# Reordering the last matmuls of a 2D prefix-sum diagonal kernel, leaving out two small sums, and making its weights by integer shifts

## The chip, the cores and the metric

The kernel runs on one core of one Trainium2 chip. The metric is the device time of one execution in microseconds (us); a smaller one is better. Times are medians over several runs. A profile is taken of one execution of each kernel; in it a span is the time from the first to the last instruction, some 1.7 us less than the device time. Ratios are the mean time of one kernel's runs over the mean of the other's runs of the same rounds, so they are not quite the ratio of the medians quoted beside them.

## The reference

```python
B, H, W = 4, 4224, 4224
def reference(x):                         # x: float32 [B, H, W]
    ps = np.cumsum(np.cumsum(x, axis=1), axis=2)
    diag = np.diagonal(ps, axis1=1, axis2=2)
    return np.cumsum(diag, axis=1).astype(np.float32)
```

Each output is a weighted sum over the matrix, so every element has to be read once, and the work on each is small.

## The kernel before

It streams each matrix as strips of 768 rows through three buffers. The last 128 rows of the last matrix come last, as four blocks of 32 rows (`part_b`, blocks 0 to 3). TensorE gathers the contributions to the last 384 outputs in one row of PSUM, `fin`, by matmuls whose left side is a column of sums. `fin_e` holds block 3's share of the last 32 outputs.

```python
    w4_ps = psum_s.tile([P, P], FP32, name="fold")        # setup
    matmul(w4_ps, quarter, weights[:R, :P], start=True)
    weights4 = consts.tile([P, P], FP32, name="weights4")
    nc.vector.tensor_copy(out=weights4, in_=w4_ps)
    # ... (four matrices of strips) ...
        by = last.tile([P, P], FP32, name="by")           # block 0, by TensorE
        nc.scalar.copy(out=by, in_=by_ps)
        weigh(arows[:, 0:1], weights, 0, start=True)      # sums of 256 earlier rows
        weigh(arows[:, 1:2], weights, P)
        weigh(ones_col, by, M0)
        weigh(dtot, weights, M0)                          # diagonal block
        for k, ca in ((0, 512), (1, 448)):                # blocks 1 and 2
            act_sum(bsum[:, k, 0:1], part_b[:, k + 1, :ca])     # ScalarE
            pair_sum(bsum[:, k, 1:2], part_b[:, k + 1, ca:])    # VectorE
            if k == 1:
                finish(0, M0)          # add the first 256 results (VectorE reads fin)
            row_sums(btot[:, k : k + 1], bsum[:, k])            # combine the two sums
            weigh(btot[:, k : k + 1], weights4, M0 + (k + 1) * R)
        act_sum(esum[:, 0:1], part_b[:, 3, :320])         # block 3
        pair_sum(esum[:, 1:2], part_b[:, 3, 320:bcut])
        pair_sum(esum[:, 2:3], part_b[:, 3, bcut:])
        for k in (1, 0, 2):
            matmul(fin_e, esum[:, k : k + 1], weights4[:, :R], start=k == 1)
        finish(M0, GW)
        # ... output of yl ...
        nc.vector.tensor_add(out=ye, in0=fin_e, in1=yl[:, E0:])   # the last addition
        # ... output of ye ...
```

Of the kernel before, what the change touches and what calls it, by code (L numbers as in the profile page):

```python
# [8 lines left out]
FP32 = mybir.dt.float32  # L9
BF16 = mybir.dt.bfloat16  # L10
I32 = mybir.dt.int32
AX = mybir.AxisListType
ALU = mybir.AluOpType
# [4 lines left out]
def kernel(  # L18
# [14 lines left out]
    nc = tc.nc  # L33
# [3 lines left out]
    P = 128  # L37
# [11 lines left out]
    consts = ctx.enter_context(tc.tile_pool(name="consts", bufs=1))  # L49
# [4 lines left out]
    last = ctx.enter_context(tc.tile_pool(name="last", bufs=1))  # L54
# [3 lines left out]
    psum_s = ctx.enter_context(  # L58
        tc.tile_pool(name="psum_s", bufs=1, space=bass.MemoryType.PSUM)
    )  # L60
# [30 lines left out]
    def upper_mask(f):  # L91
# [19 lines left out]
        out=um1,  # L111
        in_=um1,
        compare_op=ALU.is_gt,
        fill=0.0,
        base=0,
        pattern=[[1, GW]],
        channel_multiplier=-1,
# [5 lines left out]
        out=ident,  # L123
        in_=ident,
        compare_op=ALU.is_equal,
        fill=0.0,
        base=0,
        pattern=[[-1, P]],
        channel_multiplier=1,
# [8 lines left out]
    def counted(name, rows, width, pieces):  # L138

        ti = consts.tile([P, GW], I32, name="counted")[:rows, :width]  # L140
        for c0, c1, base, step, cm in pieces:
            nc.gpsimd.iota(
                ti[:, c0:c1],
                pattern=[[step, c1 - c0]],
                base=base,
                channel_multiplier=cm,
            )
        tf = consts.tile([rows, width], FP32, name=name)
        nc.gpsimd.tensor_copy(out=tf, in_=ti)
        return tf  # L150
# [6 lines left out]
    def between_groups(name, turned):  # L157
# [25 lines left out]
    weights = counted("weights", P, GW, [(0, GW, 1, 1, -1)])  # L183
    nc.gpsimd.affine_select(
        out=weights,
        in_=weights,
        compare_op=ALU.is_ge,
        fill=0.0,
        base=0,
        pattern=[[1, GW]],  # L190
        channel_multiplier=-1,
# [1 line left out]


    R = P // 4
    quarter = consts.tile([R, P], FP32, name="quarter")
    nc.gpsimd.memset(quarter, 1.0)
    for base, step in ((0, 1), (3, -1)):
        nc.gpsimd.affine_select(  # L199
            out=quarter,  # L200
            in_=quarter,
            compare_op=ALU.is_ge,
            fill=0.0,
            base=base,
            pattern=[[step, P]],
            channel_multiplier=-4 * step,
        )

    ident_h = consts.tile([P, P], BF16, name="ident_h")
    nc.vector.tensor_copy(out=ident_h, in_=ident)  # L210
# [1 line left out]
    def matmul(o, lhsT, rhs, start=False):  # L212
        nc.tensor.matmul(  # L213
            o, lhsT=lhsT, rhs=rhs, start=start, stop=False, skip_group_check=True
        )

    w4_ps = psum_s.tile([P, P], FP32, name="fold")
    matmul(w4_ps, quarter, weights[:R, :P], start=True)
    weights4 = consts.tile([P, P], FP32, name="weights4")
    nc.vector.tensor_copy(out=weights4, in_=w4_ps)  # L220
    weights4_h = consts.tile([P, P], BF16, name="weights4_h")
    nc.vector.tensor_copy(out=weights4_h, in_=w4_ps)
    ones_col = consts.tile([P, 1], FP32, name="ones_col")
    nc.vector.memset(ones_col, 1.0)

# [5 lines left out]
    def act_sum(acc, src):  # L231
        w = src.shape[-1]
        dump = dumpool.tile([P, 2176], BF16, name="dump")
        nc.scalar.activation(  # L234
            out=dump[:, :w], in_=src, func=ACT.Copy, accum_out=acc
        )

    def row_sums(acc, src):
        nc.vector.reduce_sum(out=acc, in_=src, axis=AX.X)  # L239
# [3 lines left out]
    def pair_sum(acc, src):  # L243

        w = src.shape[-1] // 2
        pair = last.tile([P, 288], FP32, name=f"pair{len(pairs)}")
        pairs.append(pair)
        nc.vector.scalar_tensor_tensor(
            out=pair[:, :w],
            in0=src[:, :w],  # L250
            scalar=1.0,
            in1=src[:, w:],
            op0=ALU.mult,
            op1=ALU.add,
            accum_out=acc,
        )
# [27 lines left out]
    dtot = last.tile([P, 1], FP32, name="dtot")  # L284
# [9 lines left out]
    for b in range(B):  # L294
# [10 lines left out]
        def row_of(j):  # L305
            return (j + t0) % NG
# [59 lines left out]
        for h in range(2):  # L366
            ps = slice(h * HP, (h + 1) * HP)
            k = row_of(h)
            nc.vector.tensor_copy(  # L369
                out=r6[ps, k : k + 2 * ns : 2, :], in_=a6[ps, :, :, 1]  # L370
# [29 lines left out]
        if not whole:  # L400
# [9 lines left out]
            for sb, c0, c1 in (  # L410
# [8 lines left out]
                    out=part_b[:, sb, c0:c1],  # L419
                    in_=x[b, r0 : r0 + R, :TB].rearrange("r (k c) -> r k c", k=4)[  # L420
                        :, :, c0:c1
                    ],
# [21 lines left out]
        for i, src in enumerate((d, c12[:, 0, :])):  # L444
            nc.vector.tensor_tensor_scan(  # L445
                out=c12[:, i, :],
# [8 lines left out]
            out=out[b, : j1 * GW].rearrange("(g i) -> g i", i=GW),  # L455
            in_=c12[t0:NG, 1, :],
# [11 lines left out]
        arows = last.tile([P, 2], FP32, name="arows")  # L468
# [3 lines left out]
        M0 = 2 * P  # L472
# [5 lines left out]
        def weigh(rows, w, r0, start=False):  # L478

            matmul(fin[:, r0:], rows, w[:, : GW - r0], start=start)  # L480

        def finish(c0, c1):
            nc.vector.tensor_add(
                out=yl[:, c0:c1], in0=fin[:, c0:c1], in1=c12[0:1, 1, c0:c1]
            )
# [5 lines left out]
            matmul(by_ps, part_b[:, 0, c : c + P], weights4_h, start=c == 0)  # L491
        by = last.tile([P, P], FP32, name="by")
        nc.scalar.copy(out=by, in_=by_ps)
        weigh(arows[:, 0:1], weights, 0, start=True)
        weigh(arows[:, 1:2], weights, P)
        weigh(ones_col, by, M0)
        weigh(dtot, weights, M0)


        bsum = last.tile([P, 2, 2], FP32, name="bsum")  # L500
        btot = last.tile([P, 2], FP32, name="btot")
        for k, ca in ((0, 512), (1, 448)):
            act_sum(bsum[:, k, 0:1], part_b[:, k + 1, :ca])
            pair_sum(bsum[:, k, 1:2], part_b[:, k + 1, ca:])
            if k == 1:
                finish(0, M0)
            row_sums(btot[:, k : k + 1], bsum[:, k])
            weigh(btot[:, k : k + 1], weights4, M0 + (k + 1) * R)


        esum = last.tile([P, 3], FP32, name="esum")
# [3 lines left out]
        for k in (1, 0, 2):  # L515
# [3 lines left out]
            out=out[b, T0 : T0 + E0].unsqueeze(0), in_=yl[:, :E0]  # L519
# [34 lines left out]
```

## Time and profile before

| | before |
|---|---|
| device time, median of 3 runs | 668.09 us (667.10 to 669.24) |
| span in the profile (an execution of 667.37 us) | 665.7 us |
| busiest compute engine, VectorE | 334.6 us, 50% |
| VectorE's setup ends, first strip's work begins | 20.95 us, 34.84 us |
| ScalarE starts on block 3 | 662.46 us |
| the last addition starts | 663.50 us |

The page's first lines and the end of the timeline are shown in the prediction. (The GB/s row there stays near 219, half of the 429 GB/s that are read; this fits the strips being stored as bf16, half as wide as the float32 input.) What it tells in words of the setup is this part of the timeline (start, duration, engine, line, operation, and in brackets the idle time of that engine before it and what ended it):

```profile
16.53 0.64 POOL L199 TENSOR_SCALAR_AFFINE_SELECT quarter<-quarter 32x128 f32<-32x128 f32 x2
17.22 0.79 PE L213 MATMUL fold<-weights,quarter 32*128 32x128 f32 x2 [17.22 <-POOL quarter L199]
18.05 0.29 DVE L220 COPY weights<-fold 128x128 f32<-128x128 f32 x1 [5.45 <-PE fold L213]
34.84 2.56 DVE L329 TENSOR_TENSOR mu<-strip,um 128x4608 bf16<-128x4608 bf16 x1 [13.89 <-DMA strip<-in_x_dram]
```

The bracket of the last line is the point: VectorE has done its setup and stands idle for 13.89 us until the first strip lands.

In this document a "tail" is the time from ScalarE's start on block 3's first piece to the start of the last addition. That ScalarE instruction waits only for its data, so it marks when the transfer has delivered it; the tail is what computing adds after that. Before, it is 663.50 - 662.46 = 1.04 us.

### The profile page before, as it was taken

The numbers are of one execution on the slowest core, as the hardware profiler recorded it, in microseconds if no ns is written. First come the engines' busy times: TensorE is split into PE (matmuls) and PEld (weight loads), VectorE is DVE, ScalarE is ACT, GpSimd is POOL, SyncE is SP. The second block draws the span as 40 slices with busy tenths as digits, with TensorE's granted clock in tenths as the row PEclk, the third lists the DMA queues.
The fourth block names the chain that finished last, engine by engine and source line by source line (L and its number), as shares of the span: only waits on it lengthen the run. The fifth ranks groups of instructions, "written<-read, shape, count | busy, mean of one in ns | idle before, by whom it ended". The sixth has DMA issues, their size and how long they took to land.

```text
span 665.7 us, 2561 instructions
## 1 busy us (share of the span) xinstructions
PE 204.8 (31%) x979; PEld 98.2 (15%) x979; DVE 334.6 (50%) x166; ACT 140.3 (21%) x226; POOL 32.0 (5%) x61
## 2 busy tenths in 40 slices
PE   0081522403117143130221623404032264250427
PEld 0030211101003021110110311202011031120103
DVE  3161625456916153454782524436288333352867
ACT  0001121406300103040630020304063002030436
POOL 7000000000000000000000000000000000001000
PEclk9995857656558585675755957666565586766758
DMA  9999999999999999999999999999999999999998
GB/s 203 219 219 219 219 218 218 219 209 212 219 221 218 218 218 219 218 218 216 209 218 220 218 216 218 219 218 218 218 213 215 219 217 215 219 217 218 218 205 161
DMA packets 7670, 143.23 MB, mean 215 GB/s; under 512 B 702, under 2 KB 1002, under 8 KB 2154
## 3 DMA queue, kind: packets, MB, share of 16 engines
q0 software_dynamic: 7296, 142.47, 99.9%
q1 hardware_dynamic: 362, 0.61, 0.3%
q8 instruction: 7, 0.11, 0.1%
q14 instruction: 5, 0.04, 0.0%
HBM read 285.47 MB, written 0.07 MB: 429 GB/s over the span
## 4 chain that ended last, share of the span: by engine, by line
DVE 47%; another core or an unknown queue 44%; DMA 5%; PE 2%; issue 1%; DVEq 0%; POOLq 0%
DVE acc L239 29%; DVE mu L329 8%; DVE strip L330 8%; DMA strip<-in_x_dram 5%; PE d L213 1%; DVE c L445 1%; PE fold L213 1%; DVE pu L239 0%; PE fin L213 0%; DVE c L259 0%; DVE rows L369 0%; DVE acc L344 0%; PE carry_ps L213 0%; DVE carry L443 0%
## 5 line engine op out<-in xcount | busy, mean ns | idle before, releaser
L213 PE MATMUL d<-strip,sel 128*11 128x384 bf16 x603 | 138.6, 403 | 359.9 <-DMA strip<-in_x_dram 359.9
L234 ACT ACTIVATE dump<-strip 128x416 bf16<-128x416 bf16 (+8 forms) x112 | 128.4, 1146 | 521.9 <-DMA strip<-in_x_dram 519.2
L329 DVE TENSOR_TENSOR mu<-strip,um 128x4608 bf16<-128x4608 bf16 (+1 forms) x24 | 52.4, 2183 | 305.8 <-DMA strip<-in_x_dram 305.7
L239 DVE TENSOR_REDUCE acc<-strip 128x6 f32<-128x4608 bf16 (+6 forms) x23 | 196.0, 8523 | 0.8
L213 PEld LDWEIGHTS <-sel 128*11 128x11 bf16 x849 | 86.2, 102 | 504.7 <-issue 463.0
L213 PE MATMUL d<-mu,sel 128*11 128x384 bf16 x243 | 49.1, 355 | 45.8 <-DVE mu L329 45.8
L330 DVE TENSOR_TENSOR strip<-strip,mu 128x4608 bf16<-128x4608 bf16 (+1 forms) x24 | 52.4, 2183 | 1.0
L76 POOL DMA_DIRECT2D strip<-in_x_dram x24 | 16.5, 688 | 542.1 <-DVE acc L239 281.5
L234 ACT ACTIVATION_READ_ACCUMULATOR dump<-strip 128x1 f32 x112 | 20.9, 186 | 0.0
L213 PE MATMUL d<-ident,rows 128*11 128x128 f32 x24 | 5.2, 380 | 16.7 <-DVE rows L378 16.7
L213 PE MATMUL fold<-strip,ident_h 128*128 128x480 bf16 x8 | 3.4, 598 | 10.6 <-DMA strip<-in_x_dram 10.6
L213 PE MATMUL fold<-weights,quarter 32*128 32x128 f32 x2 | 0.8, 496 | 17.2 <-POOL quarter L199 17.2
L213 PE MATMUL d<-halves,rows 128*11 128x64 f32 x48 | 5.6, 299 | 0.0
L94 DVE MEMSET um<- 128x4608 bf16 (+1 forms) x2 | 4.9, 2458 | 1.1 <-issue 1.1
L213 PEld LDWEIGHTS d<-halves,rows 128*11 128x11 f32 x48 | 5.1, 136 | 1.5 <-issue 1.5
L213 PEld LDWEIGHTS d<-ident,rows 128*11 128x11 f32 x24 | 2.6, 120 | 18.4 <-DVE rows L378 17.5
L95 POOL TENSOR_SCALAR_AFFINE_SELECT um<-um 128x4608 bf16<-128x4608 bf16 (+1 forms) x2 | 5.2, 2608 | 2.4 <-DVE um L94 2.4
L239 DVE TENSOR_REDUCE pu<-d 11x1 f32<-11x384 f32 x4 | 2.2, 546 | 5.2 <-PE d L213 5.2
L445 DVE TENSOR_TENSOR_SCAN c<-ones_row,carry,c 11x384 f32<-11x384 f32 x4 | 4.0, 1006 | 0.1
L445 DVE TENSOR_TENSOR_SCAN c<-ones_row,carry,d 11x384 f32<-11x384 f32 x4 | 4.0, 1000 | 0.1
L418 POOL DMA_DIRECT2D strip<-in_x_dram x5 | 2.7, 548 | 26.4 <-DMA strip<-in_x_dram 26.4
L213 PEld LDWEIGHTS <-ident_h 128*128 128x128 bf16 x14 | 1.6, 119 | 13.8 <-issue 13.5
(90 smaller groups left out, 41.5 us busy)
## 6 DMA issues: line engine op xcount, KB each, us to landing
strip<-in_x_dram POOLq DMA_DIRECT2D x19, 6336.0 KB, 76.5
strip<-in_x_dram POOLq DMA_DIRECT2D x5, 3168.0 KB, 59.7
strip<-in_x_dram POOLq DMA_DIRECT2D x1, 1080.0 KB, 49.9
strip<-in_x_dram POOLq DMA_DIRECT2D x1, 768.0 KB, 52.8
strip<-in_x_dram POOLq DMA_DIRECT2D x3, 256.0 KB, 54.0
head<-in_x_dram SPq DMA_DIRECT2D x1, 528.0 KB, 3.7
strip<-in_x_dram POOLq DMA_DIRECT2D x1, 192.0 KB, 43.2
strip<-in_x_dram POOLq DMA_DIRECT2D x1, 64.0 KB, 28.6
```

Of the source, the lines that this page charges most:

```text
L76: nc.gpsimd.dma_start(out=o, in_=x[b, r0 : r0 + f * P, :].rearrange("(p f) w -> p f w", f=f))
L94: nc.vector.memset(um, 1.0)
L95: nc.gpsimd.affine_select(out=um, in_=um, compare_op=ALU.is_gt, fill=0.0, base=0, pattern=[[-1, f], [1, f * P]], channel_multiplier=-f,)
L213: nc.tensor.matmul(o, lhsT=lhsT, rhs=rhs, start=start, stop=False, skip_group_check=True)
L234: nc.scalar.activation(out=dump[:, :w], in_=src, func=ACT.Copy, accum_out=acc)
L239: nc.vector.reduce_sum(out=acc, in_=src, axis=AX.X)
L329: nc.vector.tensor_mul(out=mu, in0=block, in1=um)
L330: nc.vector.tensor_sub(out=block, in0=block, in1=mu)
L418: nc.gpsimd.dma_start(out=part_b[:, sb, c0:c1], in_=x[b, r0 : r0 + R, :TB].rearrange("r (k c) -> r k c", k=4)[:, :, c0:c1],)
L445: nc.vector.tensor_tensor_scan(out=c12[:, i, :], data0=ones_row, data1=src, initial=carry[:, i : i + 1], op0=ALU.mult, op1=ALU.add,)
```

## The change

It is meant to shorten that tail. What is known early (diagonal, block 0) is weighed early; blocks 1 and 2 are weighed by two matmuls each, without adding their two sums first; and the weights of the setup come from an integer pattern shifted right by two bits and cut at zero, without a matmul.

```diff
+    nc.gpsimd.iota(steps, pattern=[[4, P]], base=7, channel_multiplier=-1)
+    nc.vector.tensor_single_scalar(out=steps, in_=steps, scalar=2, op=ALU.arith_shift_right)
+    nc.vector.tensor_scalar_max(out=weights4, in0=steps, scalar1=0.0)
-    # (memset and two affine_selects that make quarter)
-    matmul(w4_ps, quarter, weights[:R, :P], start=True)
-    nc.vector.tensor_copy(out=weights4, in_=w4_ps)
 ...
-        weigh(arows[:, 0:1], weights, 0, start=True)
+        weigh(dtot, weights, M0, start=True)
+        weigh(ones_col, by, M0)
+        weigh(arows[:, 0:1], weights, 0)
         weigh(arows[:, 1:2], weights, P)
-        weigh(ones_col, by, M0)
-        weigh(dtot, weights, M0)
 ...
         for k, ca in ((0, 512), (1, 448)):
             act_sum(bsum[:, k, 0:1], part_b[:, k + 1, :ca])
             pair_sum(bsum[:, k, 1:2], part_b[:, k + 1, ca:])
-            if k == 1:
-                finish(0, M0)
-            row_sums(btot[:, k : k + 1], bsum[:, k])
-            weigh(btot[:, k : k + 1], weights4, M0 + (k + 1) * R)
+        finish(0, M0)
+        for k in range(2):
+            for i in (1, 0):
+                weigh(bsum[:, k, i : i + 1], weights4, M0 + (k + 1) * R)
```

More of the change, by code (lines that the diff above doesn't have):

```diff
@@ L195 @@
     R = P // 4
-    quarter = consts.tile([R, P], FP32, name="quarter")
-    nc.gpsimd.memset(quarter, 1.0)
-    for base, step in ((0, 1), (3, -1)):
-        nc.gpsimd.affine_select(
-            out=quarter,
-            in_=quarter,
-            compare_op=ALU.is_ge,
-            fill=0.0,
-            base=base,
-            pattern=[[step, P]],
-            channel_multiplier=-4 * step,
-        )
+    steps = consts.tile([P, P], I32, name="steps")
+    nc.gpsimd.iota(steps, pattern=[[4, P]], base=7, channel_multiplier=-1)
+    nc.vector.tensor_single_scalar(
+        out=steps, in_=steps, scalar=2, op=ALU.arith_shift_right
+    )
+    weights4 = consts.tile([P, P], FP32, name="weights4")
+    nc.vector.tensor_scalar_max(out=weights4, in0=steps, scalar1=0.0)
     ident_h = consts.tile([P, P], BF16, name="ident_h")
@@ L215, in matmul @@
         )
-    w4_ps = psum_s.tile([P, P], FP32, name="fold")
-    matmul(w4_ps, quarter, weights[:R, :P], start=True)
-    weights4 = consts.tile([P, P], FP32, name="weights4")
-    nc.vector.tensor_copy(out=weights4, in_=w4_ps)
     weights4_h = consts.tile([P, P], BF16, name="weights4_h")
-    nc.vector.tensor_copy(out=weights4_h, in_=w4_ps)
+    nc.vector.tensor_copy(out=weights4_h, in_=weights4)
     ones_col = consts.tile([P, 1], FP32, name="ones_col")
@@ L493 @@
         nc.scalar.copy(out=by, in_=by_ps)
-        weigh(arows[:, 0:1], weights, 0, start=True)
+        weigh(dtot, weights, M0, start=True)
+        weigh(ones_col, by, M0)
+        weigh(arows[:, 0:1], weights, 0)
         weigh(arows[:, 1:2], weights, P)
-        weigh(ones_col, by, M0)
-        weigh(dtot, weights, M0)
         bsum = last.tile([P, 2, 2], FP32, name="bsum")
-        btot = last.tile([P, 2], FP32, name="btot")
         for k, ca in ((0, 512), (1, 448)):
```

## The prediction

> **What bounds the kernel now.** I read the head of the page first, then its slices, then the chain of waits at the end, then the timeline of the last microseconds, because only those can be touched by this change.
>
> ```profile
> PE 204.8 (31%) x979; PEld 98.2 (15%) x979; DVE 334.6 (50%) x166; ACT 140.3 (21%) x226; POOL 32.0 (5%) x61
> DMA  9999999999999999999999999999999999999998
> GB/s 203 219 219 219 219 218 218 219 209 212 219 221 218 218 218 219 218 218 216 209 218 220 218 216 218 219 218 218 218 213 215 219 217 215 219 217 218 218 205 161
> HBM read 285.47 MB, written 0.07 MB: 429 GB/s over the span
> ```
>
> No compute engine is busy more than half of the 665.7 us, while the 16 DMA engines are at nine tenths or more in every slice but the last. The input is 4 x 4224 x 4224 x 4 bytes = 285.5 MB, so each byte of it is read once, and the time is bytes over rate: 285.47 MB / 429 GB/s = 665.4 us. Hence neither the first 30 us (constants are built while the first strip arrives) nor the 600 us of strips can get shorter by having less to compute. The table of busy time by stretch says where the data ends: between 662.20 and 662.30 us the DMA engines are 0.41 busy, in the next tenth 0.13, then 0.01. So the part that computation alone decides is 662.4 to 665.7, some 3.3 us or 0.5% of the span. The timeline of VectorE, ScalarE, TensorE and the output queue at that place:
>
> ```profile
> 661.46 0.46 DVE L248 SCALAR_TENSOR_TENSOR pair<-strip 128x288 f32<-128x288 bf16 x1 [0.36 <-DMA strip<-in_x_dram]
> 661.83 0.33 PE L213 MATMUL fin<-weights,btot 128*1 128x96 f32 x2
> 662.19 0.41 DVE L483 TENSOR_TENSOR yl<-fin,c 1x256 f32<-1x256 f32 x1 [0.26 <-PE fin L213]
> 662.46 0.47 ACT L234 ACTIVATE dump<-strip 128x320 bf16<-128x320 bf16 x1 [0.27 <-DMA strip<-in_x_dram]
> 662.53 0.13 DVE L239 TENSOR_REDUCE btot<-bsum 128x1 f32<-128x2 f32 x1
> 662.60 0.37 DVE L248 SCALAR_TENSOR_TENSOR pair<-strip 128x224 f32<-128x224 bf16 x1
> 662.83 0.19 ACT L234 ACTIVATION_READ_ACCUMULATOR dump<-strip 128x1 f32 x1
> 662.90 0.28 DVE L248 SCALAR_TENSOR_TENSOR pair<-strip 128x128 f32<-128x128 bf16 x1
> 663.03 0.43 PE L213 MATMUL fin_e<-weights,esum 128*1 128x32 f32 x6
> 663.50 0.18 DVE L522 TENSOR_TENSOR ye<-fin_e,yl 1x32 f32<-1x32 f32 x1
> 663.70 0.24 SPq L523 DMA_DIRECT2D out_dram<-ye  x1
> ```
>
> Columns are start, duration, engine, line, operation. The reader is to see that ScalarE takes up the fourth block of the last rows at 662.46, when its data has come, and VectorE takes up the same piece only at 662.60: it is still adding the first 256 results (held up 0.26 us by TensorE) and a two-element sum. So VectorE is late by 0.14 us, and that is all the slack this tail has for the change to take.
>
> **What the Trainium skill says.** "Perfetto Trace Analysis", section "Identifying the Most-Contended Engine", wants a DMA-bound kernel judged by HBM utilization and not by the DMA engines' occupancy. "HBM Reference", section "Specifications (TRN2)", gives about 425 GB/s for a core that streams alone, bounded by its 16 DMA engines; this trace has 429 GB/s over the whole span, so it agrees, and nothing is left to gain while data flows. "DMA: Bandwidth & Descriptors", section "Anatomy of one DMA — SWDGE (gpsimd) path", puts a fixed cost of some 2 us on a transfer, mostly the receipt of the last byte; the last output here is issued at 663.70 and the span ends at 665.7, 2.0 us later, which agrees (this one is issued from the sync queue). The change does not touch it. "FP8 and Floating Point Precision", section "TensorE Precision Notes", gives a true fp32 matmul 4 passes. The trace shows each fp32 matmul as two records, and the two of `arows`, 640 columns in all, begin at 660.32 with the next group at 661.39: 1.07 us / 640 = 1.67 ns a column, four times the 0.42 ns that the page's 2.4 GHz would give for one pass. It agrees, and the small matmuls added here are dear for their size, though hidden.
>
> **The change, part by part.** Weights by shifts: it removes a memset and two selects on GpSimd (0.20 + 0.64 us, begun at 16.27), an fp32 matmul (0.79 us at 17.22) and a copy out of PSUM on VectorE (0.29 us); it adds an iota of 128x128 (an iota of 128x384 takes 0.44 us, so I estimate 0.2), a shift and a maximum on VectorE, estimated at 0.2 to 0.3 us each from the copies of that size (0.29 us). VectorE ends its setup about 1 us sooner than the 20.95 us of now. After that it waits for the first strip until 34.84 us, 13.89 us in all. Worth: **0 us**. GpSimd has issued the three first loads by 3.58 us and issues the next at 46.66, when TensorE has freed a buffer, so no load moves either.
>
> Order of the weights on TensorE: the sums of the diagonal block and block 0 (two fp32 matmuls of 128 columns, pitch about 0.22 us each, at 661.39 and 661.61 now) go ahead of `arows`. The copy `by` of block 0 is ready at 659.57 + 0.27 = 659.84, `arows` only at 660.27, so both fit into TensorE's idle time before it (0.79 us). The `arows` matmuls still begin at about 660.32 and still end, with about 0.17 us of drain, near 661.56; what lay behind them, 0.44 us, is gone.
>
> The early result: the addition of the first 256 results now is placed behind ten records of `fin` (the chain of waits has 660.32 to 662.17), among them block 1's, although those write other columns. In the changed program it comes ahead of blocks 1 and 2, and waits for `arows` alone, about 661.56. VectorE is then held by the sum of block 2's second part (661.46 + 0.46 + accumulator, 661.93). So the addition runs from about 661.97 to 662.36 in place of 662.19 to 662.60: **0.22 us earlier**.
>
> No combining: two additions `btot` (0.15 and 0.13 us) leave VectorE; the second of them lay right ahead of the last pieces. TensorE gets two more fp32 matmuls: by the trace 0.1 to 0.15 us of pitch each (the six records of 32 columns start within 0.24 us). Block 1's run in the gap of now 0.56 us; block 2's wait for ScalarE's sum at 662.19 and are done near 662.5, before the first of `fin_e` (662.9).
>
> What comes through: VectorE reaches the fourth block's first piece with 0.1 us to spare, and waits for its landing, at 662.46 like ScalarE: 0.14 us sooner than 662.60. The last piece follows 0.30 us later, at 662.76, and is done at about 663.05 in place of 663.19. But between stands ScalarE's sum of the same block, done at 662.83 + 0.19 = 663.02, unchanged; its `fin_e` matmul comes second of three. So the second begins at 663.06 and the third about 0.08 to 0.14 us after, ending near 663.38 against 663.46. Then `ye` and the output keep their durations. **Sum: 0.08 to 0.14 us, say 0.1 us of 668.09**, or 0.015%.
>
> **Rivals.** First, the transfer hides everything: the last 64 KB may land later than 662.76. For it: its landing has no mark of its own, since VectorE came to it late. Against: the DMA engines' share is 0.01 from 662.40. It would make the gain 0 to 0.1 us. Second, TensorE becomes the end: the four separate fp32 matmuls of blocks 1 and 2 pile up behind ScalarE's 662.19, and hold `fin_e` and the last addition back. For it: all stand in one in-order queue. Against: four times 0.15 is 0.6 at worst, while two of them have their data by 661.6; I find 0.4 us of slack. It would cost 0.1 to 0.3 us, so 668.3. Third, a shift of the load stream: a different setup on GpSimd shifts when descriptors are written or buffers come free. The trace speaks against it (three strips queued, GpSimd idle for 29.49 us before its fourth load), and each microsecond lost would show whole. Fourth, and largest, plain scatter: the three runs of before lie from 667.1 to 669.24, 2.1 us wide, twenty times the gain.
>
> **Range and chances.** Centre: 668.09 - 0.1 = 668.0; I go to 667.9, for the scatter of before is a little longer upwards. A median of three with a spread of about 1 us in single runs wanders by some 0.7 us (estimate), and so does the one that I start from: together about 1 us, so 1.4 us each way for 8 in 10, 666.5 to 669.3. A difference of 2% is 13 us, which would need a lost load or a hundred times this tail: within 2% at 0.984.
>
> **What would show it.** In the changed profile: DMA at nine tenths up to the last slice and about 429 GB/s; setup without the matmul, VectorE waiting over 13 us for the first strip; diagonal and block 0 weighed before 660.3 (relative to a span of 665.7), `yl` of 256 without a wait for TensorE; VectorE's 128x224 piece released by the DMA and level with ScalarE's 128x320; 0.1 us less from ScalarE's start on that piece (662.46 now) to `ye` (663.50 now, 1.04 us). Wrong would be: `fin_e` waiting behind `bsum` matmuls, a gap in the DMA row, or a run state that I do not see with one core.

## The result, and the profile after

| | before | after |
|---|---|---|
| device time, 6 runs each on one chip | 668.83 us (667.10 to 669.88) | 667.49 us (667.08 to 669.02) |
| ratio, 95% interval | | 0.9987 (0.9970 to 1.0004) |
| span in the profile | 665.7 us | 665.7 us |
| tail in the profile | 1.04 us | 0.98 us |

The interval holds 1, so no difference is shown. The page's first lines have not moved; TensorE has two records more, VectorE one instruction less:

```profile
PE 204.5 (31%) x981; PEld 97.8 (15%) x981; DVE 334.6 (50%) x165; ACT 140.3 (21%) x226; POOL 31.3 (5%) x59
HBM read 285.47 MB, written 0.07 MB: 429 GB/s over the span
```

The setup in the timeline of the changed kernel: the iota and the shift stand where the selects and the matmul were, VectorE is done at 19.57 us in place of 20.95, and all of it goes into a longer wait, 15.25 us in place of 13.89:

```profile
16.13 0.24 POOL L197 IOTA steps<- 128x128 int32 x1
16.40 0.23 DVE L198 TENSOR_SCALAR steps<-steps 128x128 int32<-128x128 int32 x1 [3.89 <-POOL steps L197]
34.82 2.56 DVE L320 TENSOR_TENSOR mu<-strip,um 128x4608 bf16<-128x4608 bf16 x1 [15.25 <-DMA strip<-in_x_dram]
```

The end of the timeline of the changed kernel:

```profile
659.54 0.38 PE L208 MATMUL fin<-weights,dtot 128*1 128x128 f32 x2
660.37 1.24 PE L208 MATMUL fin<-weights,arows 128*1 128x384 f32 x4
661.90 0.41 DVE L474 TENSOR_TENSOR yl<-fin,c 1x256 f32<-1x256 f32 x1
662.37 0.71 PE L208 MATMUL fin<-weights,bsum 128*1 128x96 f32 x8 [0.76 <-DVE yl L474]
662.46 0.39 DVE L239 SCALAR_TENSOR_TENSOR pair<-strip 128x224 f32<-128x224 bf16 x1 [0.15 <-DMA strip<-in_x_dram]
662.52 0.47 ACT L225 ACTIVATE dump<-strip 128x320 bf16<-128x320 bf16 x1 [0.27 <-DMA strip<-in_x_dram]
662.92 0.50 PE L208 MATMUL fin_e<-weights,esum 128*1 128x32 f32 x6
663.12 0.28 DVE L474 TENSOR_TENSOR yl<-fin,c 1x128 f32<-1x128 f32 x1
663.50 0.18 DVE L512 TENSOR_TENSOR ye<-fin_e,yl 1x32 f32<-1x32 f32 x1
```

VectorE's addition of 256 results no longer waits for TensorE, and VectorE now takes up block 3 at 662.46, released by the data, ahead of ScalarE at 662.52. That part went as meant. But look at the line of `bsum`: all eight records (block 1's and block 2's) begin at 662.37, released by VectorE's `yl`, although block 1's sums were ready before 661.1. They last until 663.08, and the second addition waits for them until 663.12, 0.60 us after ScalarE's start on block 3 (0.66 us before). Part of the time won ahead of block 3 is given back behind it.

The chain of work that ended last shows what this is worth. These are its last steps before and after (start, duration, what; the steps named "issue" and one of 0.02 us are left out):

```profile
662.72 0.27 PE fin L213 x2
663.03 0.45 PE fin_e L213 x6
663.50 0.18 DVE ye L522
```

```profile
662.37 0.73 PE fin L208 x8
663.12 0.29 DVE yl L474
663.50 0.18 DVE ye L512
```

Before, the last addition follows `fin_e`, which by the timeline ends at 663.03 + 0.43 = 663.46, 1.00 us after ScalarE's start. After, `fin_e` is done at 662.92 + 0.50 = 663.42, only 0.90 us after it, but the chain runs through the `bsum` matmuls and the second addition, and the last addition starts at 0.98. In e1 below `fin_e` ends at 0.90 too, the second addition is early, and the last one starts at 0.93. So the late second addition costs about 0.05 us (an estimate from these two profiles).

### The profile page after: what moved, and what is told of

Read it like the earlier page. It is cut to its first block, busy times and chain, and to the rows that moved or that the text cites. A ratio compares the mean times of both kernels' runs of the same rounds, so it can differ in the third digit from the quotient of the medians.

```text
span 665.7 us, 2562 instructions
## 1 busy us (share of the span) xinstructions
PE 204.5 (31%) x981; PEld 97.8 (15%) x981; DVE 334.6 (50%) x165; ACT 140.3 (21%) x226; POOL 31.3 (5%) x59
## 3 DMA queue, kind: packets, MB, share of 16 engines
HBM read 285.47 MB, written 0.07 MB: 429 GB/s over the span
## 4 chain that ended last, share of the span: by engine, by line
DVE 47%; another core or an unknown queue 45%; DMA 5%; PE 2%; issue 1%; DVEq 0%; POOLq 0%
DVE acc L230 29%; DVE mu L320 8%; DVE strip L321 8%; DMA strip<-in_x_dram 5%; PE d L208 1%; DVE c L436 1%; PE fold L208 1%; DVE pu L230 0%; DVE c L250 0%; DVE rows L360 0%; DVE acc L335 0%; PE carry_ps L208 0%; DVE pair L239 0%; PE fin L208 0%
## 5 line engine op out<-in xcount | busy, mean ns | idle before, releaser
L230 DVE TENSOR_REDUCE parts<-strip 128x3 f32<-128x3072 bf16 x1 | 3.4, 3353 | 0.0
```

Of the source, the lines that this page charges most:

```text
L230: nc.vector.reduce_sum(out=acc, in_=src, axis=AX.X)
```

## The experiments

Two theories were to be told apart. **Hidden:** the transfer sets the time and the change moves under 0.1 us. **Real gain:** the 0.13% of the first comparison is there, and comes from the setup or from the tail. A second question was why TensorE's `bsum` matmuls start late, and a third came up on the way: the clock of TensorE.

### e1, the kernel before against itself

No edit.

> The kernel before against itself: what the timing can't tell apart. Hidden-behind-the-transfer theory: ratio 1.000 within about 0.0015, so that the 0.9987 of the first comparison is within scatter. Rival (the 0.13% is a real gain): the ratio here is within 0.0005 of 1 and that of the changed kernel in the same rounds stays below 0.999. In the profile, the time from ScalarE's start on the 128x320 piece to the last addition's start is 1.04 us again, within 0.03.

The median was 667.40 us against 668.76 for its twin, ratio 0.9996 (0.9977 to 1.0015). Two copies of one kernel can thus differ by 1.36 us in their medians, as much as the change "won". The tail was 0.93 us, not 1.04: outside what I expected. In this execution TensorE began `arows` earlier relative to the data (2.34 us ahead of ScalarE's start on block 3, against 2.14), so the addition of 256 was held up less (0.14 us after VectorE's sum in place of 0.26). The tail of the kernel before is 0.93 to 1.04 us, by the run.

### e2, the changed kernel again

No edit.

> The changed kernel once more, same chip and rounds as its twin of before. Hidden theory: ratio 0.999 to 1.001, no difference to the twin's own ratio beyond the scatter. Rival (real gain): about 0.9987. Profile: ScalarE's 128x320 to the last addition 0.98 us within 0.03 (1.04 before); the eight records of block 1 and 2 sums start only after the addition of 256 results has ended.

The median was 668.51 us, ratio 1.0010 (0.9990 to 1.0030); the tail 0.97 us, with the eight `bsum` records again released by `yl`. The 0.9987 did not come back. This is against the real gain.

### e3, the setup alone

```diff
     # before, with only the weights by iota, shift and maximum
```

> Only the weights by shifts, all else as before. Hidden theory: ratio 1.000 within 0.0015, VectorE waits about 15.2 us for the first strip in place of 13.9, and the first strip's work still begins at 34.8 us; tail 1.04 us. Rival (the setup is what gains): 0.9987.

The ratio was 0.9992 (0.9975 to 1.0008), the tail 0.99 us, not the 1.04 expected. VectorE waited 14.79 us for a first strip that came at 34.36, somewhat earlier than in the kernel before. Nothing is shown to come from the setup.

### e4, the tail alone

```diff
     # after, with the weights by the matmul as before
```

> Only the new order and the separate matmuls; weights by the matmul as before. Hidden theory: ratio 1.000 within 0.0015 (0.06 us of 668 is 0.9999); tail 0.98 us within 0.03, VectorE waits 13.9 us for the first strip. Rival (the tail gains): 0.9987.

The ratio was 0.9993 (0.9976 to 1.0009). But the profiled execution had a tail of 1.86 us, twice what I expected, with this in the timeline of TensorE and VectorE:

```profile
660.56 0.58 PE L213 MATMUL fin<-weights,dtot 128*1 128x128 f32 x2
661.37 2.34 PE L213 MATMUL fin<-weights,arows 128*1 128x384 f32 x4
663.74 0.41 DVE L483 TENSOR_TENSOR yl<-fin,c 1x256 f32<-1x256 f32 x1 [0.80 <-PE fin L213]
664.21 0.71 PE L213 MATMUL fin<-weights,bsum 128*1 128x96 f32 x8 [0.50 <-DVE yl L483]
```

The same four records of `arows` take 2.34 us in place of 1.24. The table of stretches has the reason in its clock column (after the busy times of the five engines come the granted TensorE clock, the DMA share and GB/s):

```profile
653.80:660.40 6.60, 4.45 (x40) 2.51 (x39) 5.65 (x11) 5.04 (x9) 0.00 (x0) 1.00 1.09 210
660.60:663.80 3.20, 3.11 (x9) 0.60 (x8) 1.39 (x7) 2.02 (x7) 0.00 (x0) 0.50 0.56 96
```

The granted clock, 1.00 until 660.4, is 0.50 from 660.6 to 663.8, so TensorE becomes the engine that the tail waits for (VectorE's addition of 256 stands idle 0.80 us for it).

### e5, new order and early addition, with combining

```diff
     # before, with the new order of weigh(), and
+        finish(0, M0)
+        for k in range(2):
+            row_sums(btot[:, k : k + 1], bsum[:, k])
+            weigh(btot[:, k : k + 1], weights4, M0 + (k + 1) * R)
```

> Setup and two-element additions as before; only the order of the weighing and the early addition of 256 results. Measured from ScalarE's start on the 128x320 piece to the start of the last addition. Theory (the matmuls of blocks 1 and 2 wait until VectorE has read the first 256 results, whatever the columns, because all are in one tile): the two-element additions stand again between the addition of 256 and VectorE's 128x224 piece, so that piece starts about 0.15 us later than in the changed kernel, and four fin records, not eight, follow; 1.0 us within 0.04. Rival (order alone brings the whole gain): 0.98 or less with VectorE's piece level with ScalarE's.

670.45 us (one run), tail 1.82 us: the clock had fallen here too, at 661.63 us, and neither expectation came. As a test of the order it is inconclusive, since TensorE's slow `arows` records decide everything after them.

### e6, separate matmuls in the old order

```diff
     # before, with
-            row_sums(btot[:, k : k + 1], bsum[:, k])
-            weigh(btot[:, k : k + 1], weights4, M0 + (k + 1) * R)
+            for i in (1, 0):
+                weigh(bsum[:, k, i : i + 1], weights4, M0 + (k + 1) * R)
```

> Only the matmuls without combining; order, place of the addition of 256 and setup as before. Theory: block 1's four records lengthen what the addition of 256 waits for, by 0.1 to 0.3 us against 662.19 - 662.46 = -0.27 us relative to ScalarE's 128x320 piece, so VectorE is late on the last pieces; last addition at 1.05 to 1.2 us. Rival (no pile-up, separate is cheaper by itself): at most 0.98.

670.47 us (one run), tail 2.54 us, again with the clock fallen (at 661.4). Both expectations missed. Here VectorE's addition of 256 waits longest:

```profile
663.86 0.63 PE L213 MATMUL fin<-by,ones_col 128*1 128x128 f32 x2
664.29 0.63 PE L213 MATMUL fin<-weights,dtot 128*1 128x128 f32 x2
665.31 0.41 DVE L483 TENSOR_TENSOR yl<-fin,c 1x256 f32<-1x256 f32 x1 [1.82 <-PE fin L213]
```

`by` and `dtot`, at half clock, stand behind `arows` and ahead of what `yl` waits for. In e4, which differs from e6 in the order and the place of the addition alone, they are done before. The tails differ by 2.54 - 1.86 = 0.68 us. So the new order seems to be worth some tenths of a microsecond where the clock has fallen; the size is not settled, since it is one profile of each and the clock came back 0.4 us later, relative to the data, in e6.

### e7, the row of results in two PSUM tiles

```diff
-        fin = psum_s.tile([1, GW], FP32, name="fin")
+        fin_a = psum_s.tile([1, M0], FP32, name="fin_a")     # first 256 results
+        fin_b = psum_s.tile([1, P], FP32, name="fin_b")      # last 128
     # weigh() writes to each what belongs there; finish() reads one of them
```

> The changed kernel with its row of 384 results in two PSUM tiles, 256 and 128 wide (one more matmul for each of arows). Theory (one tile makes the sums of blocks 1 and 2 wait for VectorE's read of the first 256): the first bsum matmuls now start some 0.7 us ahead of that read's end, all are done near +0.15 us after ScalarE's 128x320 start in place of +0.57, the second addition starts at +0.55 in place of +0.60 and the last at 0.92 to 0.95 us. Rival (they wait for something else, ScalarE's sum or the queue): no record moves by more than 0.1 us. Time: ratio 1.000 within 0.002 in either case.

The ratio was 1.0003 (0.9977 to 1.0028). The clock fell at 659.41 us in the profile, the tail was 1.40 us, and the `bsum` matmuls stood behind slow `arows` records until 0.18 us after ScalarE's start on block 3, so the expected times did not come. The question of what they wait for is answered all the same:

```profile
663.05 0.41 DVE L478 TENSOR_TENSOR yl<-fin_a,c 1x256 f32<-1x256 f32 x1 [0.72 <-PE fin_a L208]
663.07 0.72 PE L208 MATMUL fin_b<-weights,bsum 128*1 128x96 f32 x8
```

With only the tile split, and the `arows` matmuls with it, the `bsum` matmuls begin 0.02 us after VectorE's read of the first 256 results has begun, and not after its end at 663.46.

### e8, two tiles and a smaller share for ScalarE

```diff
     # e7, and
-        act_sum(esum[:, 0:1], part_b[:, 3, :320])
-        pair_sum(esum[:, 1:2], part_b[:, 3, 320:bcut])
+        act_sum(esum[:, 0:1], part_b[:, 3, :256])
+        pair_sum(esum[:, 1:2], part_b[:, 3, 256:bcut])
-        for k in (1, 0, 2):
+        for k in (0, 1, 2):
```

> As the one with two tiles, and ScalarE sums 256 columns of the last block's first piece in place of 320, its matmul first of the three. Theory (ScalarE's sum is then what the last matmuls wait for): the last addition starts 0.05 to 0.1 us sooner again, 0.85 to 0.9 us after ScalarE's start on that piece. Rival: VectorE's pieces set it, no change. Time: not to be told from before, ratio 1.000 within 0.002; this is the shortest tail that I can build from the change.

Here the clock held. TensorE and VectorE in the timeline of this kernel:

```profile
661.37 0.49 PE L208 MATMUL fin_b<-weights,bsum 128*1 128x96 f32 x4
662.08 0.53 PE L208 MATMUL fin_b<-weights,bsum 128*1 128x64 f32 x4 [0.22 <-DVE pair L239]
661.95 0.41 DVE L478 TENSOR_TENSOR yl<-fin_a,c 1x256 f32<-1x256 f32 x1
663.14 0.34 PE L208 MATMUL fin_e<-weights,esum 128*1 128x32 f32 x6 [0.53 <-ACT dump L225]
```

Block 1's matmuls now run at 661.37, before VectorE reads the first 256 results, and block 2's begin while it reads them (661.95 to 662.36). In the one-tile kernel both waited for that read. So it is the shared tile that makes them wait, not the sums and not TensorE's queue (e7 shows it without the other share of ScalarE). The tail was 0.93 us, not the 0.85 to 0.90 that I expected: I had put ScalarE's matmul first of the three, and TensorE stood idle 0.53 us, until ScalarE's sum came; VectorE's first had been ready since 662.95, 0.19 us before that matmul began. Ratio 0.9999 (0.9965 to 1.0033).

### e9, a load in the setup

```diff
+    for _ in range(36):
+        nc.vector.memset(idle, 0.0)          # 128x1024 bf16
```

> The changed kernel with 36 useless fills of 128x1024 bf16 on VectorE in the setup, about 31 us by the 0.85 ns per element of the fills in the trace. Hidden theory: VectorE begins the first strip about 16 us late, the fourth load is issued about 16 us late, at some 63 us, while the three first strips keep the transfer busy to about 92 us: ratio 1.000 within 0.002. Rival (the setup lies on the path): up to 16 us longer, ratio 1.024; if part of it counts, in between.

The fills were shorter than I took them for: each is recorded as 128x512 of uint32, 0.48 us with 0.17 us behind it, so 36 of them make 23.6 us, not 31. The fourth load was issued at 53.77 us in place of 46.66:

```profile
53.77 0.78 POOL L76 DMA_DIRECT2D strip<-in_x_dram  x1 [37.37 <-DVE acc L234]
```

VectorE began the first strip at 43.10 us in place of 34.82. The time did not change: 668.64 us against 668.53 for the kernel before in the same rounds, ratio 1.0001 (0.9979 to 1.0023). A setup that is 23.6 us longer, and the strips' work 8.3 us later, cost nothing that this timing resolves; nor is a gain to be expected from one that is 1.4 us shorter.

### e10, a load in the tail

```diff
+        for _ in range(5):
+            nc.vector.memset(idle, 0.0)
         ye = last.tile([1, R], FP32, name="ye")
```

> The changed kernel with 5 such fills right before the last addition, about 4.4 us. Theory (the last 3.3 us are decided by computation alone): the time grows by 4.0 to 4.4 us, ratio 1.006 to 1.0066, so a true tail gain of 1 us would be near the limit of what the timing tells and 0.06 us far below it. Rival (the end is hidden too): no change.

The last addition came 3.98 us after ScalarE's start on block 3 in place of 0.98, so 3.0 us were put in (not the 4.0 to 4.4 expected: the fills were short here too). The time was 671.37 us against 668.53 for the kernel before, 2.84 us more; ratio 1.0042 (1.0023 to 1.0060). Within this interval the tail counts in full, as the theory has it. The interval's half width, 0.0019 or 1.2 us, is what this timing resolves: twenty times the 0.06 us of the change.

### e11, one strip less to read

```diff
-            if strip is None:
+            if strip is None and (b, s) == (1, 1):
+                strip = kept                 # work on the strip before again
+            elif strip is None:
```

> Wrong result on purpose: the second strip of the second matrix is not loaded, the first is worked on again. All computing stays, 12.98 MB of 285.47 are not read. Transfer theory: 12.98 MB / 429 GB/s = 30.3 us less, about 637 to 638 us. Rival (computing or the waits for buffers set the pace): less than 15 us shorter.

The result is wrong on purpose (relative error 0.22). 639.47 us (one run) against 668.53 for the kernel before: 29.1 us less, where bytes over rate said 30.3, with the computing unchanged (VectorE is busy for 334.6 us as before):

```profile
HBM read 272.50 MB, written 0.07 MB: 427 GB/s over the span
```

So the time follows the bytes.

### e12, TensorE kept busy

```diff
+        def spin(n):                         # after the last strip only
+            for _ in range(n):
+                matmul(warm, ident_h, um6[:, 0, :512], start=True)   # result unused
     # spin(1) ahead of carry_ps, spin(3) behind it,
     # spin(1) behind fold_a's last part, spin(1) behind block 0's matmuls
```

> The changed kernel with six useless bf16 matmuls of 512 columns (about 0.21 us each at full clock) put into TensorE's idle gaps of the last 9 us, result unused. In 4 of the 12 profiles so far the granted TensorE clock fell from 1.0 to 0.5 about 6.8 us after it had risen, in the middle of the tail, and those tails are 0.4 to 1.6 us longer; in the others it held to the end of the matmuls. Clock theory (TensorE's idle gaps let the clock fall): the clock stays at 1.0 from its rise to the last matmul, ScalarE's 128x320 piece to the last addition is 0.98 us within 0.05, and span end minus that start is 3.1 to 3.2 us. If the fallen clock made most of the 2 to 3 us scatter of the times, the runs now lie within 1 us of each other and the ratio is near 0.999; rival (the scatter is where the transfer ends, 662.3 to 664.75 us in the profiles): they still lie over 667 to 670, ratio 1.000 within 0.0015.

The clock stayed at 1.0 from its rise to the last matmul, the tail was 0.92 us (just under the 0.93 to 1.03 expected), and span end minus ScalarE's start 666.7 - 663.6 = 3.1 us. The runs lie from 667.39 to 668.40 us, within 1.01 us, against 667.68 to 671.20 for the kernel before in the same rounds; medians 667.79 and 668.81, ratio 0.9978 (0.9962 to 0.9995). This is the only interval that lies below 1. But the clock had also held in 8 of the first 12 profiles, in all four of the changed kernel with or without a load among them, so one more profile in which it holds does not show that the added matmuls held it. The two stretches that matter, the 3.4 us up to the fall in e4 and the like stretch here, which the clock outlived (the first figure after the length is TensorE's busy time):

```profile
657.11:660.52 3.41, 1.78 (x17) 0.90 (x15) 2.92 (x7) 2.23 (x6) 0.00 (x0) 1.00 1.11 208
```

```profile
658.79:662.21 3.42, 3.16 (x21) 1.22 (x20) 2.80 (x6) 2.86 (x7) 0.00 (x0) 1.00 1.05 190
```

TensorE was busy for 1.78 of 3.41 us there and for 3.16 of 3.42 us here; in e3, though, the clock outlived a stretch with 1.76 us. That a fallen clock makes the late runs later fits all profiles: in the four where it fell (e4 to e7) the tail is 1.40 to 2.54 us, in the others without an added load 0.92 to 1.04. That it makes most of the scatter is not shown. ScalarE's start on block 3 alone lies between 662.30 and 664.75 us over the profiles, and only one execution of each kernel is profiled. Six quiet runs may also be luck in part: e3, without these matmuls, had five within 1.4 us. And e12 was timed against the kernel before only, not against the changed one.

## Why the prediction was right or wrong

**The time.** 667.9 us was predicted, 667.49 measured, within the range 666.5 to 669.3, and the class "within 2%" came. That it came within 0.4 us is luck: the same kernel gave 668.51 in e2. The reason given holds, but not by the sum given for it: 285.47 MB over 429 GB/s must give the span, since that rate is those bytes over that span. What shows it is e11, where the time follows the bytes, with e9.

**The setup, worth nothing.** Right. It ended 1.38 us sooner (predicted about 1), all of it added to the wait for the first strip; e3 and e9 bear it out. The iota took 0.24 us (estimate 0.2), shift and maximum 0.23 us each (0.2 to 0.3).

**The order on TensorE.** Right at full clock: diagonal and block 0 began at 659.54 and 659.97, `arows` at 660.37, hardly moved.

**The early addition, and VectorE level with ScalarE on block 3.** Right: 661.90 (predicted about 661.97), and VectorE released by the data 0.06 us ahead of ScalarE.

**"Block 1's run in the gap of now 0.56 us".** This step failed. The matmuls of block 1 ran with those of block 2 after `yl` had been read, and the second addition waited for all eight, to 0.60 us after ScalarE's start on block 3. Without that wait it could have begun at the end of VectorE's last sum, as in e1, at 0.49. The prediction's sum for the end followed `fin_e` to the last addition and had the second addition nowhere in it; the chain after the change ran through just that. I had seen in the profile of before that `yl` waited for a matmul on other columns of `fin`, and did not turn the argument round: if VectorE's read waits for any write to the tile, a later write waits for the read as well. The Trainium skill has a reason for such a guard ("PSUM — Partial Sum Buffer", section "PSUM bank collisions raise a hardware error"): two engines must not touch one bank and quadrant at the same time, at whatever address. The waits in these traces agree, and e7 and e8, where two tiles let TensorE write while VectorE reads, were correct; in which banks the tiles lie, no trace here shows. The second rival of the prediction, TensorE holding the last addition back, was thus real, by another cause than ScalarE's late sum, and cost about 0.05 us, not 0.1 to 0.3.

**The sum, "0.08 to 0.14 us".** Too large by at least a little: 1.04 - 0.98 = 0.06 us between the first two profiles, and with the repeats nothing clear. The end of `fin_e` came 1.00 - 0.90 = 0.10 us sooner, so that part of the sum came true in these two profiles; the late second addition took 0.04 us of it. At full clock the tails of kernels with the old order are 1.04, 0.93 and 0.99 us (before, e1, e3), those of the changed one 0.98, 0.97 and 0.99 (after, e2, e9). The base was mis-sized too: the 0.14 us by which VectorE came late were a matter of one execution (0.14, 0.09 and -0.06 us in before, e3 and e1).

**The passes of a float32 matmul.** The prediction's 1.67 ns a column can be set against a bf16 matmul of these traces: three of 512 columns in e12 take 0.82 us in all and 0.38 us each, so they start 0.22 us apart, 0.43 ns a column. The ratio of 3.9 agrees with the four passes.

**The scatter.** Its size was judged well, the word "plain" was not. The profiles show two candidates: where the transfer ends (662.30 to 664.75 us for the last block), and whether the clock of TensorE holds. The prediction took every duration of the tail from one trace at full clock and had no rival in which the clock fell. There the change may be worth more than predicted (e4 against e6), but no timing here shows it.

## What to carry to other kernels

When a transfer sets the time, first find the short stretch after the last byte and work out the gain from there alone; then ask whether the timing can resolve it, by putting a known load at that place and one elsewhere (here 3.0 us in the tail cost 2.84 us, 23.6 us in the setup cost nothing that could be measured). Results that are read early should not share a PSUM tile with results that are still being written (here worth some hundredths of a microsecond at most, and no timing shows it). And a tail read from one trace holds for that trace's clock and arrival of data only: repeat the unchanged kernel before tenths of a microsecond are believed.

## What the Trainium skill lacked or had wrong

- "TensorE: Matmul & The Clock Gate", section "What's actually happening": the page lets the clock fall after an idle window of about 3.4 us and does not say how idle; it also tells of a kernel whose frequent micro-idle stretches made the clock swing, without a figure. Here it fell with no TensorE gap above 0.69 us in the 3.41 us before (e4), after stretches in which TensorE was busy for 1.66 to 1.82 us (e4 to e7). It held in stretches with 2.2 to 3.2 us. A busy time of 1.76 us (e3) and one of 1.85 us (e10) were outlived, so no sharp bound is shown; a figure of this kind is what the page lacks. The 3.4 us that it gives for its window agree: the clock fell about 6.8 us after its rise in e4 to e7, twice the window, and, after the last matmul, 10.2 us in the kernel before and 13.7 us in e1, three and four windows.
- None of the pages used here tells how far the end of a stream of loads wanders: the last block's landing lay 2.45 us apart, of some 663, over the profiles of kernels that load the same and differ in a few instructions. On the rate of a core that streams alone, the page that the prediction cites agrees with the 429 and 427 GB/s measured.
